# Seven-product FFN blocks from the second f block on, with GpSimd making their sums

## The chip, the cores and the metric

The kernel runs on one NeuronCore of a Trainium2 chip. The metric is the device time of one execution in microseconds (us). The engines have their names from the profile: PE (TensorE matmul) and PEld (its weight loads), DVE (VectorE), ACT (ScalarE), POOL (GpSimd) and SP (SyncE, which here only issues DMAs). SBUF is the on-chip memory, PSUM the accumulator that matmuls write.

## The reference, cut to what matters

The reference is two layers of a hybrid decoder: 16 learned tokens and 512 real ones (528 in all), width 1024, with an attention group and a retention group of heads in each layer and then a feed-forward part. The change touches the feed-forward part alone:

```python
hn = rmsnorm(h, ffn_norm_g)
ff = silu(hn @ w_gate) * (hn @ w_up)       # 1024 -> 2816, twice
return h + ff @ w_down                     # 2816 -> 1024
```

Layer 0 computes it for all 528 tokens, layer 1 only for the 512 real ones. All is float32. The kernel gets float32 accuracy from fast matmuls by splitting each operand into a high part (a rounded cast) and a low part (the rest): a product is three matmuls, high x high, high x low and low x high.

## The kernel before, in words

**Layout.** The residual `h` lies in SBUF as eight tiles `h[0..7]` of 128 features x 528 tokens. The 2816 hidden features of the FFN are 22 blocks of 128, called f blocks. For each f block, a gate matrix and an up matrix of 1024 x 128 are needed, each loaded by SP as one tile of 128 x 8 x 128.

**Plain f blocks** (`f < PLAIN`, lines 1031 to 1034). `dense_steps` (line 197) makes eight steps for the gate and eight for the up, one for each 128 input features: in layer 0 a step is six matmuls of 264 columns (three products, two halves of the tokens), in layer 1 three of 512. A block is 96 or 48 matmuls. The weights are cast by ACT (`whi`, line 191), and the low parts are made by DVE or, with `pool=True`, by POOL in eight pieces of 128 columns (line 194). Weights of the next matrix are made ahead at steps 1 and 4 of the current one. The high and low weight tiles are rings of two buffers.

**Seven-product f blocks** (class `Unit`, line 887). Gate and up are taken together as a 2 x 2 product of blocks: the 1024 inputs in two halves (rows), the tokens in two halves (columns). A Winograd form does it with seven half-size products in place of eight: 84 matmuls of 264 columns (256 in layer 1) for gate and up together. It needs sums of inputs and sums of weights:

- The token sums: `x_forms(k)` (line 834) for k = 0 to 3 makes, from `h[k]` and `h[k+4]`, four sums and differences in a tile `S`, and splits them into `th` (ACT) and `tl` (DVE). These serve all units of the layer. `S` is a ring of two buffers, so the third form can be started only when the first is split.
- The weight sums: `make1` to `make4` (lines 907 to 928). `make2` adds the two halves of up into `S[HB:NK]`, subtracts the gate's half, and splits the result (`splits`, lines 867 to 869); its tile comes from the same ring `S`. `make3` overwrites half of up in place.

A unit runs its `head` (24 matmuls on the ordinary inputs, no sums), its `middle` (36 matmuls on the token sums and on the tiles of `make2` and `make3`) and its `tail` (24). `need(j)` (line 862) makes a job's weights and those of up to two jobs after it when the first matmul of a product is reached. Round 0 holds f blocks 0 to 2; before the change all three are plain (`PLAIN = 3`), the units begin at f = 3, and from there on pieces of the down projection of the round before are put between the units.

**What sets the order.** PE runs in the order in which the Python steps are called. The other engines' orders are laid out by a planner at build time, by program order as priority, its own costs and the time at which tiles come free; after that each engine runs its queue strictly in order. The FFN's tiles lie in the memory that the attention tiles of the layer held.

**The start of the FFN.** `start_ffn` makes the scaled high and low inputs `xh`, `xl` (lines 311 to 324) from `h`. `ffn` then returns its list of steps, into which the last lines (1216 to 1220) insert other work by position: the squares for the norm before step 4; the norm (`rstd`, four or two matmuls), the held gate of block 0 and form 0 before step 12; forms 1, 2 and 3 before steps 20, 28 and 36. So the forms are spread over the three plain blocks.

Of the kernel before, what the change touches and what calls it, by code (L numbers as in the profile page):

```python
# [16 lines left out]
NK = D // 128  # L17
# [7 lines left out]
DFF = 2816  # L25
NF = DFF // 128
ROUNDS = ((0, 3), (3, 7), (7, 11), (11, 15), (15, 19), (19, 22))
PLAIN = 3
HB = NK // 2
EPS = 1e-6  # L30
NBLK = SEQ // 128
# [8 lines left out]
def hybrid_kernel(ctx, tc, x_t, w_in, w_fl, w_out, w_gate, w_up, w_down, vecs, b_fg, rope, decay, mask, ident, out_t):  # L40
# [232 lines left out]
    def fft(tag, dt=F32R, shape=(128, T), bufs=None):  # L273
        return phase["ffn"].tile(list(shape), dt, name=tag, tag=tag, bufs=bufs)
# [518 lines left out]
    def ffn(l, st, real, last):  # L793
# [14 lines left out]
        def g_done(f):  # L808
            def go(ps):
                sg = tt("sg")  # L810
                if isinstance(ps, list):
                    for v, (c0, c1) in zip(ps, QC):
                        nc.vector.scalar_tensor_tensor(sg[:, c0:c1], v[:, 0:c1 - c0], RSC, st["R"][:, c0:c1],
                                                       ALU.mult, ALU.mult)
                else:
                    nc.vector.scalar_tensor_tensor(sv(sg, real), pv(ps, real), RSC, sv(st["R"], real), ALU.mult, ALU.mult)
                silu(sv(sg, real))
                sgs[f] = sg
            return go

        def u_done(f):
            def go(ps):
                u = tt("tq")
                nc.vector.scalar_tensor_tensor(sv(u, real), pv(ps, real), RSC, sv(st["R"], real), ALU.mult, ALU.mult)
                nc.vector.tensor_mul(sv(u, real), sv(u, real), sv(sgs[f], real))
                fh, fl = act_tile(f)
                split(sv(fh, real), sv(fl, real), sv(u, real))
                acts[f] = (fh, fl)
            return go
# [4 lines left out]
        def x_forms(k):  # L834
            def go():
                if k == 0:
                    st["t"] = [[fft(f"t{p}{i}", shape=(128, 2, 4, w)) for p in "hl"] for i in range(2)]
                s = fft("S", F32, (128, 6, w), 2)
                a, b = ((h[k][:, c0:c1], h[HB + k][:, c0:c1]) for c0, c1 in HC)
                g0, g1 = vcol(V_FFN + l * NK + k), vcol(V_FFN + l * NK + HB + k)  # L840
                nc.scalar.activation(s[:, 0:2], two(h[k]), AF.Copy, scale=g0)
                nc.vector.tensor_sub(s[:, 2], s[:, 1], s[:, 0])
                for i in range(2):
                    nc.vector.scalar_tensor_tensor(s[:, 3 + i], b[1], g1, s[:, 1 + i], ALU.mult, ALU.subtract)
                nc.vector.scalar_tensor_tensor(s[:, 5], a[1], g1, s[:, 4], ALU.mult, ALU.subtract)
                th, tl = (t[:, k % 2] for t in st["t"][k // 2])
                split(th, tl, s[:, 2:6])
            return go
# [38 lines left out]
        class Unit:  # L887
# [23 lines left out]
            def make2(self, hi, lo):  # L911
                a, b = self.t["a"], self.t["b"]
                s = self.t["s"] = fft("S", F32, (128, NK, 128), 2)
                nc.vector.tensor_add(s[:, HB:NK], b[:, 0:HB], b[:, HB:NK])
                nc.vector.tensor_sub(s[:, 0:HB], s[:, HB:NK], a[:, 0:HB])
                splits(hi, lo, s)

# [111 lines left out]
        for r, (f0, f1) in enumerate(ROUNDS):  # L1029
            for f in range(f0, f1):  # L1030
                if f < PLAIN:
                    steps += dense_steps(w_gate[l, f], [(0, xs, NK, QC, g_done(f) if f else held.append)], banks=f == 1)
                    steps += dense_steps(w_up[l, f], [(0, xs, NK, QC, u_done(f))])
                    continue
                u = Unit(f)
                steps += u.head()
                for v in tails:
                    v.last()
                    steps += v.tail()
                tails = []  # L1040
                u.rest()
                steps += u.middle()
                if fills:
                    p, g0, g1 = fills.pop(0)
                    j = down_job(p, g0, g1)
                    steps += down(j, 0, 2 * p, g0, g1, not real)
                    u.last()
                    steps += u.tail()
                    steps += down(j, 1, 2 * p + 1, g0, g1, False)
                else:  # L1050
                    tails = [u]
            for p, g0, g1 in fills:
                j = down_job(p, g0, g1)
                for s in range(2):
                    steps += down(j, s, 2 * p + s, g0, g1, False)
            fills = [(p, f0, f1) for p in range(NK // 2)]
# [6 lines left out]
        else:  # L1063
# [149 lines left out]
            places = [(end, after_a)] + [(end + n * (i + 1), f) for i, f in enumerate(  # L1213
                (after_0, after_1, after_2, after_3, after_4, after_5, after_6, after_7))]
            steps += merge(rnd, places)
        for i in range(HB):
            steps.insert(NK + 4 + 9 * i, x_forms(i))
        steps.insert(NK + 4, lambda: g_done(0)(held[0]))
        steps.insert(NK + 4, lambda: rstd(st, QC))
        steps.insert(4, lambda: squares(st, QC, False, False))  # L1220
        return steps

    gf = const.tile([128, NK], F32, name="gf")
    nc.vector.tensor_scalar_mul(gf, vec[:, V_FIN:V_FIN + NK], RSC)
# [180 lines left out]
```

## Time and profile before

| | |
|---|---|
| median of 3 runs | 1274.08 us (1273.74 to 1275.27) |
| the profiled execution | 1278.19 us; its span 1276.3 us; mean granted PE clock 0.995 |
| first gate matmul of the FFN, layer 0 / layer 1 | 290.0 us / 918.0 us |
| three plain f blocks, layer 0 | from 290.0 to 325.6 us |
| POOL's additions of line 194 | 504 instructions, 259.9 us |
| POOL's busy time from 345 to 620 us (units of layer 0) | 0.38 us |
| DVE's busy time from 345 to 620 us | 220.33 us of 275 |
| DVE's busy time from 284 to 326 us | 41.93 us of 42 |

The profile is one execution. Its chain of work follows the wait that ended last at each point back from the end; the groups sum equal instructions with the mean time of one; the timeline and the windows show a stretch in order of time, in us from the span's start. In a timeline row the first number is the start, the second the time that it took; DVE instructions of 128 x 528 are listed with 0.70 us but start 0.62 us apart, since the next one starts before the last is written out. The ends of matmuls are modelled, so their starts are what to count by.

### The profile page before, as it was taken

What the parts mean: (1) busy time and instruction counts of PE and PEld (TensorE: products, weight loads), DVE (VectorE), ACT (ScalarE), POOL (GpSimd) and SP (SyncE); (2) the same over time, 40 slices, a digit from 0 to 9 for tenths busy, and PEclk for the clock granted to TensorE, in tenths of its full rate; (3) what the DMA queues carried; (4) which work ended last, traced back from release to release, by engine and by line L of the source; (5) the groups of instructions that cost most, each with busy time, mean ns of one, the idle gap of its engine ahead of it and who ended that gap; (6) DMA issues with size and microseconds to landing.
All of it is one profiled execution on the core that took longest, in us unless ns stands there. A gap on an engine that the chain in (4) does not pass through costs nothing.

```text
span 1276.3 us, 23615 instructions
## 1 busy us (share of the span) xinstructions
PE 1258.8 (99%) x9271; PEld 1199.9 (94%) x9271; DVE 996.6 (78%) x1843; ACT 688.2 (54%) x1246; POOL 265.2 (21%) x522
## 2 busy tenths in 40 slices
PE   9999999999999999999999999999999999999997
PEld 8899999999999999999998989999789999999996
DVE  7777856779988887887785777567899888888866
ACT  6666545676444444444464665456764444444444
POOL 3355546420000000000025545554100000000000
PEclk9999999999999999999999999999999999999998
DMA  6322232223333333332323232232224333333321
GB/s 216 93 68 84 79 94 72 74 67 112 108 96 100 100 100 100 100 100 83 102 74 100 76 100 84 75 92 67 99 86 129 100 100 100 100 99 101 106 76 67
DMA packets 45680, 120.57 MB, mean 94 GB/s; under 512 B 5360, under 2 KB 12272, under 8 KB 45568
## 3 DMA queue, kind: packets, MB, share of 16 engines
q1 hardware_dynamic: 45136, 118.77, 29.8%
q8 instruction: 73, 1.20, 0.4%
q14 instruction: 39, 0.32, 0.1%
q10 hardware_dynamic: 432, 0.29, 0.1%
HBM read 116.91 MB, written 2.13 MB: 93 GB/s over the span
## 4 chain that ended last, share of the span: by engine, by line
PE 94%; DVE 2%; ACT 1%; DMA 1%; issue 0%; DVEq 0%; ACTq 0%; SPq 0%
PE psd L217 30%; PE psa L880 18%; PE psd L1015 14%; PE psd L880 13%; PE psa L217 5%; PE psa L1015 4%; PE psa L418 2%; PE psa L572 2%; PE psa L507 2%; PE psa L729 1%; PE psa L699 1%; DMA bc<-cdr 1%; PE psa L379 1%; PE psa L290 0%; DMA cdr<-z 0%
## 5 line engine op out<-in xcount | busy, mean ns | idle before, releaser
L194 POOL TENSOR_TENSOR wlo<-raw,whi 128x128 fp32r<-128x128 f32 x504 | 259.9, 551 | 293.5 <-ACT whi L191 293.5
L217 PE MATMUL psd<-xh,whi 128*128 128x264 f32 (+1 forms) x792 | 197.1, 316 | 0.6 <-ACT whi L191 0.6
L217 PE MATMUL psd<-xh,wlo 128*128 128x264 f32 (+1 forms) x792 | 187.7, 305 | 0.0
L217 PE MATMUL psd<-xl,whi 128*128 128x264 f32 (+1 forms) x792 | 187.3, 304 | 0.4 <-DVE xl L320 0.4
L217 PEld LDWEIGHTS psd<-xh,whi 128*128 128x128 f32 x792 | 129.4, 191 | 5.7 <-ACT whi L191 1.3
L217 PEld LDWEIGHTS psd<-xh,wlo 128*128 128x128 f32 x792 | 128.0, 190 | 6.4 <-DVE wlo L194 0.4
L217 PEld LDWEIGHTS psd<-xl,whi 128*128 128x128 f32 x792 | 128.6, 190 | 4.8 <-DVE xl L320 0.8
L191 ACT CAST whi<-raw 128x512 fp32r<-128x512 f32 (+1 forms) x168 | 98.5, 614 | 51.6 <-PE psd L217 38.2
L868 ACT CAST whi<-raw 128x1024 fp32r<-128x1024 f32 (+2 forms) x62 | 54.9, 886 | 51.0 <-PE psd L880 39.5
L868 ACT CAST fwhi<-raw 128x1024 fp32r<-128x1024 f32 (+2 forms) x62 | 55.7, 898 | 46.6 <-PE psd L880 39.2
L1115 POOL TENSOR_TENSOR th<-th,e 128x544 f32<-128x544 f32 x1 | 1.4, 1370 | 359.1 <-DVE e L1135 359.1
L85 POOL MEMSET kl<- 64x528 f32 x2 | 1.1, 534 | 345.4 <-PE psa L880 345.4
L869 DVE TENSOR_TENSOR wlo<-raw,whi 128x1024 fp32r<-128x1024 f32 (+2 forms) x62 | 62.9, 1015 | 12.1 <-ACT whi L868 12.0
L869 DVE TENSOR_TENSOR fwlo<-raw,fwhi 128x1024 fp32r<-128x1024 f32 (+2 forms) x62 | 64.0, 1032 | 9.6 <-ACT fwhi L868 9.5
L880 PE MATMUL psa<-th,whi 128*128 128x264 f32 (+1 forms) x232 | 65.4, 282 | 0.0
L880 PE MATMUL psa<-th,wlo 128*128 128x264 f32 (+1 forms) x232 | 65.4, 282 | 0.0
L880 PE MATMUL psa<-tl,whi 128*128 128x264 f32 (+1 forms) x232 | 65.3, 282 | 0.0
L880 PE MATMUL psa<-th,fwhi 128*128 128x264 f32 (+1 forms) x224 | 63.4, 283 | 0.0
L880 PE MATMUL psa<-tl,fwhi 128*128 128x264 f32 (+1 forms) x224 | 63.3, 283 | 0.0
L880 PE MATMUL psa<-th,fwlo 128*128 128x264 f32 (+1 forms) x224 | 63.2, 282 | 0.0
L527 ACT ACTIVATE probs<-probs,nmax 128x144 f32<-128x144 f32 (+1 forms) x64 | 36.9, 577 | 47.3 <-DVE nmax L514 34.5
L868 ACT CAST fwhi<-S 128x1024 fp32r<-128x1024 f32 x20 | 21.0, 1050 | 69.1 <-PE psa L880 67.1
(340 smaller groups left out, 4053.7 us busy)
## 6 DMA issues: line engine op xcount, KB each, us to landing
raw<-w_in SPq DMA_DIRECT2D x54, 512.0 KB, 3.5
raw<-w_gate SPq DMA_DIRECT2D x44, 512.0 KB, 3.8
fraw<-w_up SPq DMA_DIRECT2D x38, 512.0 KB, 3.5
raw<-w_down SPq DMA_DIRECT2D x64, 256.0 KB, 2.8
raw<-w_out SPq DMA_DIRECT2D x16, 512.0 KB, 3.4
raw<-w_down SPq DMA_DIRECT2D x32, 192.0 KB, 2.5
bc<-cdr SPq DMA_DIRECT2D x16, 264.0 KB, 3.4
raw<-w_up SPq DMA_DIRECT2D x6, 512.0 KB, 3.6
```

The lines of the kernel that those rows point to most:

```text
L191: pin(nc.scalar.copy(hi, job["raw"][:, c0:c1]), pinned)
L194: pin(sub(lo[:, i:i + step], job["raw"][:, c0 + i:c0 + i + step], hi[:, i:i + step].bitcast(F32)), pinned)
L217: nc.tensor.matmul(ps[1][b][:, 0:c1 - c0], w[:, wk, :], x[:, c0:c1], start=(k == 0 and i == 0), stop=(k == n - 1 and i == 2))
L379: nc.tensor.matmul(ps[:, 0:c1 - c0], wf[:, k, :], st["x"][k][part][:, c0:c1], start=(i == 0), stop=(i == 2 * NK - 1))
L418: nc.tensor.transpose(ps[:, 128 * j:128 * j + 128], src[:, o:o + 128], idt)
L507: nc.tensor.matmul(sc[0:nq, 0:c1 - c0], st["q"][s][:, q0:q0 + nq], kk[:, c0:c1], start=(i == 0), stop=(i == 1))
L527: nc.scalar.activation(pr, pr, AF.Exp, bias=nmax[0:nq], scale=-1.0, accum_out=rsum)
L572: nc.tensor.matmul(po[:, c0:SEQ], v[:, j, :], pp[:, j, META + c0:T], start=(j == 0 and i == 0), stop=(j == 4 and i == 1))
L868: nc.scalar.copy(hi, src)
L869: nc.vector.tensor_sub(lo, src, hi.bitcast(F32))
L880: nc.tensor.matmul(bank()[:, 0:b.shape[-1]], a[:, o + k, :], b, start=(fresh and k == 0 and i == 0), stop=(k == n - 1 and i == 2), skip_gr ...
L1015: nc.tensor.matmul(v[:, 0:c1 - c0], a[:, s * n + k, :], b[:, c0:c1], start=(k == 0 and i == 0), stop=(k == n - 1 and i == 2))
```

## The change

`PLAIN` goes from 3 to 1: f blocks 1 and 2 of each layer become units, so four blocks in all. The four forms are now placed before steps 5, 7, 9 and 11 of the one plain block (16 steps), and the norm before step 11. In a form, ACT scales both `h[k]` and `h[k+4]` into `S` (which has eight parts now), and the four sums are subtractions of 264 or 256 columns on POOL; before, they were one subtraction and three fused operations on DVE. The plain block's up has its low parts made by POOL, eight pieces of 128 columns. In `make2` of every unit (42 now, 38 before) the sum of the up halves is four POOL additions of 128 columns in place of one DVE addition of 512. Transfers and their sizes stay as they were.

```diff
-PLAIN = 3
+PLAIN = 1
...
-                s = fft("S", F32, (128, 6, w), 2)
-                a, b = ((h[k][:, c0:c1], h[HB + k][:, c0:c1]) for c0, c1 in HC)
+                s = fft("S", F32, (128, 8, w), 2)
                 g0, g1 = vcol(V_FFN + l * NK + k), vcol(V_FFN + l * NK + HB + k)
                 nc.scalar.activation(s[:, 0:2], two(h[k]), AF.Copy, scale=g0)
-                nc.vector.tensor_sub(s[:, 2], s[:, 1], s[:, 0])
+                nc.scalar.activation(s[:, 6:8], two(h[HB + k]), AF.Copy, scale=g1)
+                nc.gpsimd.tensor_sub(s[:, 2], s[:, 1], s[:, 0])
                 for i in range(2):
-                    nc.vector.scalar_tensor_tensor(s[:, 3 + i], b[1], g1, s[:, 1 + i], ALU.mult, ALU.subtract)
-                nc.vector.scalar_tensor_tensor(s[:, 5], a[1], g1, s[:, 4], ALU.mult, ALU.subtract)
+                    nc.gpsimd.tensor_sub(s[:, 3 + i], s[:, 7], s[:, 1 + i])
+                nc.gpsimd.tensor_sub(s[:, 5], s[:, 6], s[:, 4])
                 th, tl = (t[:, k % 2] for t in st["t"][k // 2])
                 split(th, tl, s[:, 2:6])
...
                 s = self.t["s"] = fft("S", F32, (128, NK, 128), 2)
-                nc.vector.tensor_add(s[:, HB:NK], b[:, 0:HB], b[:, HB:NK])
+                for i in range(HB):
+                    nc.gpsimd.tensor_add(s[:, HB + i], b[:, i], b[:, HB + i])
                 nc.vector.tensor_sub(s[:, 0:HB], s[:, HB:NK], a[:, 0:HB])
                 splits(hi, lo, s)
...
                 if f < PLAIN:
-                    steps += dense_steps(w_gate[l, f], [(0, xs, NK, QC, g_done(f) if f else held.append)], banks=f == 1)
-                    steps += dense_steps(w_up[l, f], [(0, xs, NK, QC, u_done(f))])
+                    steps += dense_steps(w_gate[l, f], [(0, xs, NK, QC, g_done(f) if f else held.append)], f > 0, f == 1)
+                    steps += dense_steps(w_up[l, f], [(0, xs, NK, QC, u_done(f))], True)
...
-        for i in range(HB):
-            steps.insert(NK + 4 + 9 * i, x_forms(i))
-        steps.insert(NK + 4, lambda: g_done(0)(held[0]))
-        steps.insert(NK + 4, lambda: rstd(st, QC))
-        steps.insert(4, lambda: squares(st, QC, False, False))
-        return steps
+        forms = (5, 7, 9, 11)
+        return merge(steps, [(4, lambda: squares(st, QC, False, False)), (NK + 3, lambda: rstd(st, QC)),
+                             (NK + 3, lambda: g_done(0)(held[0]))], [(p, x_forms(i)) for i, p in enumerate(forms)])
```

## The prediction

> **What bounds the kernel now.** I read the page first: the busy shares, the slices, the chain that ended last.
>
> ```profile
> PE 1258.8 (99%) x9271; PEld 1199.9 (94%) x9271; DVE 996.6 (78%) x1843; ACT 688.2 (54%) x1246; POOL 265.2 (21%) x522
> ...
> DVE  7777856779988887887785777567899888888866
> ...
> POOL 3355546420000000000025545554100000000000
> ...
> PE 94%; DVE 2%; ACT 1%; DMA 1%; issue 0%; DVEq 0%; ACTq 0%; SPq 0%
> ```
>
> PE is the bound: 94% of the chain is its own work. So fewer matmuls gain what they take, and work shifted between DVE and POOL gains nothing unless PE waited for it; it can cost. DVE is fullest (9 tenths) where each FFN starts; POOL does nothing in the FFNs. Next I read the chain of waits in time over the start of the FFN, layer 0 and then layer 1 (start, length, what).
>
> ```profile
> 302.58 5.79 PE psa L217 x48
> 308.37 17.36 PE psd L217 x144
> 325.73 1.45 PE psa L880 x12
> ...
> 918.05 1.14 ACT whi L191 x2
> 919.19 1.24 ACT S L841 x2
> 920.43 0.61 ACT xh L319
> ...
> 930.66 5.52 PE psa L217 x24
> 936.19 16.59 PE psd L217 x72
> 952.77 1.43 PE psa L880 x12
> ```
>
> L217 is a plain block, L880 a unit. In layer 0 PE runs three plain blocks without a wait of note; in layer 1 ACT's scaled copies for two forms stood ahead of `xh` and reached the chain.
>
> **The gain in matmuls.** Layer 0: 144 plain matmuls take 17.36 us, 0.1206 each; a block of 96 takes 11.57. Twelve unit matmuls take 1.45; the 84 take 10.15. Gain 1.42 a block, 2.8 for two. Layer 1: 72 in 16.59 is 0.2304, a block of 48 takes 11.06; 7 x 1.43 = 10.01; gain 1.05 a block, 2.1 for two. Together 4.9 us, 0.4% of the kernel, if PE never waits.
>
> **When PE wants the first weight sums.** Before, unit 3 came behind three plain blocks; now unit 1 comes behind one. Its head (24 matmuls, 2.9 us) needs no sums; its middle needs all four token sums and the tile of `make2`. In layer 0 block 1 began at 302.58, so the middle is wanted at 305.5; in layer 1 block 1 began at 930.66, plus 2.85: 933.5.
>
> **When POOL can have them.** POOL gets 8 low parts of the plain up, 16 subtractions, and 4 additions of `make2`, in program order. The source view and the groups of instructions give POOL's prices:
>
> ```profile
> L194 POOL TENSOR_TENSOR wlo<-raw,whi x504: 447/463/2071, 21.9 to 902.8; 128x128 fp32r<-128x128 f32 x168
> L1115 POOL TENSOR_TENSOR th<-th,e 128x544 f32<-128x544 f32 x1 | 1.4, 1370 | 359.1 <-DVE e L1135 359.1
> ```
>
> The timelines of ACT and DVE give the earliest start and the other links:
>
> ```profile
> 289.98 1.15 ACT L191 CAST whi<-raw 128x512 fp32r<-128x512 f32 x2 [0.63 <-PE psd L217]
> 291.03 0.74 ACT L841 ACTIVATE S<-h,vec 128x528 f32<-128x528 f32 x1
> 300.31 1.07 ACT L142 CAST th<-S 128x1056 fp32r<-128x1056 f32 x1
> 322.83 1.06 ACT L868 CAST fwhi<-S 128x1024 fp32r<-128x1024 f32 x1 [1.03 <-DVE S L915]
> 301.42 1.26 DVE L143 TENSOR_TENSOR tl<-S,th 128x1056 fp32r<-128x1056 f32 x1
> 322.11 0.69 DVE L915 TENSOR_TENSOR S<-S,raw 128x512 f32<-128x512 f32 x1
> 323.92 1.23 DVE L869 TENSOR_TENSOR fwlo<-S,fwhi 128x1024 fp32r<-128x1024 f32 x1
> ```
>
> One piece of 128 columns is 0.45 to 0.46 us undisturbed (447 least, 463 median). 264 columns on POOL are not in the trace. Between 463 ns at 128 and 1370 at 544 a column costs 2.18 ns, so 264 cost an estimated 0.76 and 256 0.74. Bounds: 0.46, the same price as 128, and 1.37, the row of 544; I take the value between, which the two rows fix.
>
> [...]
>
> The up's cast could begin at 289.98 because PE had then let go of the weight ring; ACT copied the first form's `S` only behind it, at 291.03, with gaps in its queue before. So I read the FFN's `S` memory as coming free with the last out projection. Walk in layer 0, POOL never disturbed:
> - 8 low parts from 290.6, when half of the cast is done: 8 x 0.45, to 294.2.
> - Forms 0 and 1: 4 x 0.76 = 3.04 each, to 297.2 and 300.2.
> - Form 2 needs form 0's buffer: `th` 1.07 and `tl` 1.26 after 297.2, then its copy 0.74: 300.3. It runs to 303.3, form 3 to 306.3.
> - `make2` of unit 1 needs a buffer of `S` too, the one of form 2 (305.7), and stands behind form 3: 4 x 0.45 to 308.1; DVE's subtraction 0.69, ACT's cast 1.06: high part at 309.9; low part 1.23 later, 311.1.
>
> PE issues two matmuls with the high part (0.24 us) and stops for the low: wanted at 305.7, there at 311.1. Loss 5.4. In layer 1 the same walk, from 918.6 (the cast began at 918.05) with 0.74 a sum, ends at 938.9 against 933.7: 5.2. So undisturbed POOL alone loses 10.6 us, more than twice the gain.
>
> **POOL disturbed.** DVE is full there (window over the plain block of layer 0: span, then PE, PEld, DVE, ACT, POOL busy), and POOL and DVE are seen to hold each other up (their timelines in the attention, the group of all POOL pieces, DVE's timeline ahead of the gate):
>
> ```profile
> 290.02:302.20 12.18, 12.18 (x101) 12.03 (x100) 12.14 (x22) 7.94 (x14) 0.00 (x0) 1.00 0.63 212
> 85.09 4.42 POOL L194 TENSOR_TENSOR wlo<-raw,whi 128x128 fp32r<-128x128 f32 x6 [4.62 <-ACT whi L191]
> 86.57 0.85 DVE L758 TENSOR_TENSOR d<-d,sg 128x528 f32<-128x528 f32 x1
> 87.34 0.96 DVE L452 TENSOR_TENSOR kl<-tq,kh 64x528 fp32r<-64x528 f32 x1
> 88.23 0.96 DVE L297 TENSOR_TENSOR nwt<-r 128x528 f32<-128x528 f32 x1
> L194 POOL TENSOR_TENSOR wlo<-raw,whi 128x128 fp32r<-128x128 f32 x504 | 259.9, 551 | 293.5 <-ACT whi L191 293.5
> 291.09 2.12 DVE L320 SCALAR_TENSOR_TENSOR xl<-h,vec,xh 128x528 fp32r<-128x528 f32 x3
> 293.75 1.44 DVE L320 SCALAR_TENSOR_TENSOR xl<-h,vec,xh 128x528 fp32r<-128x528 f32 x2
> ```
>
> Six POOL pieces that should take 2.7 us take 4.42, and DVE's neighbours, all with two SBUF inputs, follow each other 0.77 to 0.89 us apart. Over the kernel a POOL piece takes 551 ns on average, 0.09 over the median: 28 instructions pay 2.5 us. The other end is that each meets a DVE instruction and waits some 0.3 to 0.4 more: 28 x 0.35 is 9.8. DVE has less to do than before (the twelve fused operations are gone), but what remains, `xl`, `tl` and weight lows, has two SBUF inputs. I take 3 us a layer, near the mean row. The other way DVE pays: the last two `xl` (1.44 us from 293.75) were just in time for PE, and the POOL pieces now beside them may delay gate steps by about 1 us; that stays in the range, as do 0 to 1.3 us for two more `S` copies ahead of `xh` in ACT's queue.
>
> [...]
>
> **PE's clock.** A PE that stands still runs slower afterwards:
>
> ```profile
> 680.00:686.00 6.00, 3.61 (x16) 2.78 (x15) 3.99 (x15) 2.96 (x11) 1.70 (x4) 0.79 0.34 117
> ```
>
> With PE idle for 2.4 of 6 us the granted clock averaged 0.79, a loss of about 0.21 x 6 = 1.3 us of matmul time. For a stop of 8 us I add 1.5 in each layer; from 0 (it falls while PE stands anyway) to 3.
>
> **What costs nothing.** The later units hide their POOL additions (a steady unit of layer 0: DVE's, ACT's and PE's rows):
>
> ```profile
> 501.98 0.69 DVE L914 TENSOR_TENSOR S<-fraw 128x512 f32<-128x512 f32 x1 [0.72 <-DMA fraw<-w_up]
> 508.24 1.05 ACT L868 CAST fwhi<-S 128x1024 fp32r<-128x1024 f32 x1 [4.20 <-PE psa L880]
> 512.39 1.46 PE psa L880 x12
> ```
>
> The addition starts when its load lands, 6.3 us before ACT may cast (it waits for a weight buffer from PE), and PE needs it after the head (2.9 us from 512.39), 13 us on. Four additions of 0.45, or 3.2 if each is disturbed as above, and the 0.69 of the subtraction fit. Queued behind that subtraction on DVE are `make3` in place (it must also let the additions read first) and evictions; were the cover gone, each of 38 units would pay up to 3 us. DVE's relief (an addition of some 0.69 a unit, the form work) frees no PE wait. The weight loads are the same bytes; those of units 1 and 2 replace the plain blocks' in the same places.
>
> **The sum.** Gain 4.9; walk 10.6; disturbance 2 x 3 = 6.0; clock 2 x 1.5 = 3.0: 10.6 + 6.0 + 3.0 - 4.9 = 14.7 us slower. On the profiled execution's 1278.19 that is 1292.9; that execution lies 4.1 above the median of 1274.08, so the median comes to 1288.8.
>
> **The rivals.**
> - *Faster: the sums are there in time.* If the `S` memory is free before 290, ACT copies forms 0 to 2 as their `h` arrive and POOL, idle at that point, does 9 us of subtractions ahead of the gate. It decides at POOL's first subtraction: from some 5.4 us before the walk's 294.2, so at about 289, the wait is gone. For it: the out projection completes most tiles of `h` before the gate begins. Against it: in both layers ACT copied `S` only behind the up's casts. Time: 1274.1 - 4.9 = 1269.2. Chance 0.15.
> - *No change.* The sums come 2.5 us late in each layer (a cheaper POOL column: the lower bound of 0.46 takes 16 x 0.30 = 4.8 off a layer's walk, and disturbance gives about half of it back): 1274. Chance 0.06.
> - *Units bound by their sums.* The POOL additions, each held up by DVE's long low-part instructions, push `make2` past ACT's slot in every unit: some 0.4 us in each of 42 on top of the forecast, 17 us: 1306. For it: DVE at 8 tenths there. Against it: the 4.2 us that ACT waits. Chance 0.05.
> - That the change does not do what it says can be left out: the count of matmuls follows from the steps.
>
> **How the numbers follow.** Forecast 0.74: slower by 6 (no disturbance, no clock: 10.6 - 4.9) to 28 us (9.8 a layer, 3 a layer of clock), so 1280 to 1302. The range goes down to 1272, taking in no change, and leaves out most of the faster case and of the last. Differences below 0.2% (2.5 us) are about what a measurement of this kernel cannot tell from none. Faster 0.15, same 0.06, slower 0.79.
>
> **What would show it.** In the profile after: PE idle ahead of the first L880 on `th` with the weights of `S`, some 5 to 11 us in each layer, its releaser ACT's cast or DVE's low part of `S`; POOL busy without a gap from about 291 to 310 with pieces well over 0.46; POOL subtractions of 264 near 0.76; a drop of the granted clock behind the wait; units from f = 3 on without PE waits. I am wrong if POOL's subtractions begin before 289, or if PE has no wait there.

## The result, and the profile after

The changed kernel takes 1315.88 us (median of 4 runs, 1314.7 to 1317.35) against 1274.67 for the kernel before on the same chip: a ratio of 1.0323, 95% interval 1.0305 to 1.0341. It is 41 us slower. The prediction was 14.7 slower, with a range that ended at 1302. The direction was right and the size was not.

The profiled execution took 1317.35 us, with a span of 1315.6. Below are the page's busy line, two of the slice lines and the engines' shares of the chain, as they were shown of the kernel before.

```profile
PE 1265.8 (96%) x9319; PEld 1206.9 (92%) x9319; DVE 989.1 (75%) x1792; ACT 701.8 (53%) x1266; POOL 428.0 (33%) x738
...
POOL 3445645436222111110034545454442111211100
PEclk9999999997999999999999999999978999999999
...
PE 83%; DVE 7%; POOL 3%; ACT 3%; issue 1%; DMA 1%; DVEq 0%; ACTq 0%; SPq 0%; POOLq 0%
```

PE's own work went from 94% to 83% of the chain; DVE, POOL and ACT stand on it now. The clock has a dip at the start of each layer's FFN. PE's matmuls date the loss. From the first gate matmul to the first down product (the first matmul of the down projection), a stretch with the same three f blocks and the head and middle of unit 3, the profiled executions took:

| us | layer 0 | layer 1 |
|---|---|---|
| before | 42.79 | 41.64 |
| after | 59.29 | 59.37 |
| from the first down product to the FFN's end, before | 314.87 | 304.47 |
| the same, after | 316.51 | 310.44 |

That is 16.5 + 17.7 in the first stretch and 1.6 + 6.0 behind it, 41.8 of a difference of 39.2 between the two profiled executions; the other stretches are 2.6 shorter. So the loss is where the prediction looked, but more than twice as large in each layer (7.1 was predicted for layer 0: 5.4 + 3 + 1.5 - 2.8).

The windows view over that stretch (us, then busy us and instructions of PE, PEld, DVE, ACT and POOL, then the granted clock, DMA share and GB/s), layer 0, before and after:

```profile
290.02:332.81 42.79, 42.79 (x355) 42.64 (x354) 42.38 (x70) 26.48 (x39) 0.00 (x0) 1.00 0.38 120
```

```profile
288.68:347.97 59.29, 44.51 (x330) 43.20 (x329) 45.45 (x57) 33.48 (x48) 33.48 (x40) 0.86 0.27 85
```

Read the first row twice: PE was busy for all of 42.79 us, and DVE for 42.38 of them. Two engines were full, and the swap of the blocks takes work from one of them only. Afterwards neither is full; everything waits on something. PE's rows that have a wait ahead of them from unit 1 on, from the timeline of layer 0 after:

```profile
303.24 0.39 PE L880 MATMUL psa<-xh,wlo 128*128 128x264 f32 x1 [0.90 <-DVE wlo L869]
...
314.36 0.56 PE L880 MATMUL psd<-xh,whi 128*128 128x264 f32 x1 [9.63 <-DVE sg L816]
...
319.70 0.59 PE L880 MATMUL psa<-th,fwhi 128*128 128x264 f32 x1 [2.36 <-ACT fwhi L868]
...
321.76 0.59 PE L880 MATMUL psa<-th,fwlo 128*128 128x264 f32 x1 [1.25 <-DVE fwlo L869]
```

The long stop is one that the prediction did not have: unit 1's head wants a PSUM bank for its `z` tile, and the bank is still held by block 0's gate, which waits for the norm `R`. The wait for the weight sums that the prediction described comes behind it, 2.4 + 1.3 us. In layer 1 PE stops 10.63 us for the same bank and then finds the sums just made. The chain that ended last shows why both are late (start, length, what):

```profile
289.39 6.73 POOL wlo L194 x8
296.12 0.71 POOL S L842
296.83 1.44 POOL S L844 x2
...
300.10 0.74 ACT S L841
...
300.91 2.90 POOL S L844 x2
...
304.66 1.07 ACT th L142
305.73 0.75 ACT R L295 x2
306.49 0.63 ACT S L841
...
307.19 1.92 POOL S L844 x2
...
309.94 1.08 ACT th L142
...
311.05 1.26 DVE tl L143
312.31 1.17 DVE R L300
...
313.50 0.71 DVE sg L816
```

The chain runs through POOL's forms into ACT's `th` and DVE's `tl`, and from `tl` straight into `R` at 312.31: the norm does not need the forms, but it stands behind them in ACT's and DVE's queues. ACT's second copy of a form, `S` of line 841, stands behind `th` in the same way, and POOL waits for it.

### The profile page after: what moved, and what is told of

Same layout as the page of the kernel before. It is cut to its first block, busy times and chain, and to the rows that moved or that the text cites. A ratio compares the mean times of both kernels' runs of the same rounds, so it can differ in the third digit from the quotient of the medians.

```text
span 1315.6 us, 23991 instructions
## 1 busy us (share of the span) xinstructions
PE 1265.8 (96%) x9319; PEld 1206.9 (92%) x9319; DVE 989.1 (75%) x1792; ACT 701.8 (53%) x1266; POOL 428.0 (33%) x738
## 4 chain that ended last, share of the span: by engine, by line
PE 83%; DVE 7%; POOL 3%; ACT 3%; issue 1%; DMA 1%; DVEq 0%; ACTq 0%; SPq 0%; POOLq 0%
PE psd L217 23%; PE psa L880 19%; PE psd L880 13%; PE psd L1016 13%; PE psa L1016 4%; PE psa L217 4%; PE psa L418 2%; PE psa L572 2%; PE psa L507 1%; PE psa L729 1%; PE psa L699 1%; POOL S L844 1%; POOL wlo L194 1%; POOL S L915 1%; PE psa L379 1%
## 5 line engine op out<-in xcount | busy, mean ns | idle before, releaser
L194 POOL TENSOR_TENSOR wlo<-raw,whi 128x128 fp32r<-128x128 f32 x520 | 272.5, 558 | 323.9 <-ACT whi L191 323.8
L915 POOL TENSOR_TENSOR S<-fraw 128x128 f32<-128x128 f32 x168 | 121.3, 753 | 447.9 <-DMA fraw<-w_up 424.4
L217 PE MATMUL psd<-xh,whi 128*128 128x264 f32 (+1 forms) x720 | 177.8, 316 | 0.5 <-ACT whi L191 0.5
L217 PE MATMUL psd<-xl,whi 128*128 128x264 f32 (+1 forms) x720 | 168.7, 303 | 1.4 <-DVE xl L320 1.4
L217 PE MATMUL psd<-xh,wlo 128*128 128x264 f32 (+1 forms) x720 | 168.1, 302 | 0.0
L217 PEld LDWEIGHTS psd<-xl,whi 128*128 128x128 f32 x720 | 116.4, 190 | 6.1 <-DVE xl L320 3.2
L217 PEld LDWEIGHTS psd<-xh,whi 128*128 128x128 f32 x720 | 117.1, 191 | 4.7 <-ACT whi L191 1.2
L217 PEld LDWEIGHTS psd<-xh,wlo 128*128 128x128 f32 x720 | 115.8, 189 | 4.8
L880 PE MATMUL psa<-th,wlo 128*128 128x264 f32 (+1 forms) x264 | 75.1, 284 | 0.3 <-DVE wlo L869 0.3
L880 PE MATMUL psd<-xh,whi 128*128 128x264 f32 (+1 forms) x176 | 51.6, 293 | 20.3 <-DVE sg L816 20.3
L947 ACT COPY e<-psa 128x264 f32<-128x264 f32 (+1 forms) x126 | 47.3, 375 | 33.6 <-PE psa L880 27.7
```

The lines of the kernel that those rows point to most:

```text
L194: pin(sub(lo[:, i:i + step], job["raw"][:, c0 + i:c0 + i + step], hi[:, i:i + step].bitcast(F32)), pinned)
L217: nc.tensor.matmul(ps[1][b][:, 0:c1 - c0], w[:, wk, :], x[:, c0:c1], start=(k == 0 and i == 0), stop=(k == n - 1 and i == 2))
L880: nc.tensor.matmul(bank()[:, 0:b.shape[-1]], a[:, o + k, :], b, start=(fresh and k == 0 and i == 0), stop=(k == n - 1 and i == 2), skip_gr ...
L915: nc.gpsimd.tensor_add(s[:, HB + i], b[:, i], b[:, HB + i])
L947: nc.scalar.copy(self.t["e"][:, i], self.t["x"][:, 0:w])
```

## The experiments

Four causes were weighed. P, the prediction's own: POOL's sums are late and its instructions and DVE's hold each other up. D: DVE was already full, and a unit gives it more work than a plain block. G, the hand-over: the last unit of round 0 ends its activations too late for the first down product, because its tail is put off into the next unit. C, the queues: work that needs no sums waits in order behind `th` and `tl`, which wait for POOL. Each ratio is to the kernel before on the same chip in the same session, and a difference of two runs in us is that of their ratios, or of their times where they were taken together.

### Is it POOL at all?

plain1_dve keeps one plain block and the new positions, and does everything on DVE as before.

```diff
-PLAIN = 3
+PLAIN = 1
...
+        forms = (5, 7, 9, 11)
```

> One plain block per layer and the forms at steps 5 to 11 as in the change, but every sum and low part on DVE as before; POOL does nothing in the FFN. Theory A (POOL's chain, stretched by DVE, makes the sums late): DVE alone needs from 295.7 us about 1.2 (lows) + 6.2 (forms) + 4.7 (tl) + 3.7 (norm, held gate) + 1.1 + 2.3 (weights of unit 1) = 19 us, so the first weight sums come some 9 us late instead of the change's 16 to 18: about 1288, some 25 us under the change. Theory B (PE stops for the PSUM bank of the held gate, wherever the sums are made): the norm still queues behind four forms, so nearly the same stop: 1308 to 1316.

Measured: 1308.61 us, ratio 1.0260 (1.0243 to 1.0277). The same swap loses 33 us with no work on POOL. The time is one that theory B named, but not by its mechanism: PE's wait for the held gate's bank is down to 3.40 us in layer 0, and 6.08 + 0.45 us are waits for the weight sums. The window of layer 0's stretch, and DVE's rows around the first weight sum:

```profile
288.90:342.76 53.86, 43.93 (x330) 42.99 (x329) 49.87 (x78) 30.47 (x44) 0.00 (x0) 0.90 0.29 94
```

```profile
309.26 2.42 DVE L143 TENSOR_TENSOR tl<-S,th 128x1056 fp32r<-128x1056 f32 x2
311.60 0.70 DVE L143 TENSOR_TENSOR al<-tq,ah 128x528 fp32r<-128x528 f32 x1
312.22 1.28 DVE L914 TENSOR_TENSOR S<-fraw 128x512 f32<-128x512 f32 x2
313.42 0.68 DVE L915 TENSOR_TENSOR S<-S,raw 128x512 f32<-128x512 f32 x1
```

DVE has 49.87 us to do where it had 42.38, and it runs without a gap of note until 321.7; unit 1's sum waits its turn there and is done at 314, where PE wanted it at about 309. forms_dve takes the changed kernel and puts only the forms back on DVE; the up's low parts and the additions stay on POOL.

```diff
-                nc.gpsimd.tensor_sub(s[:, 2], s[:, 1], s[:, 0])
+                nc.vector.tensor_sub(s[:, 2], s[:, 1], s[:, 0])
...
```

> The change with the four forms back on DVE (the six-part S); the up's low parts and the weight sums stay on POOL. Theory A: POOL's chain shrinks from 28 us to 8 lows (6.7) and 4 additions (2.8), DVE takes 6.2 us of forms: first sums some 9 to 10 us late, about 1288 to 1292. Theory B: as the change, 1308 to 1316.

Measured: 1309.74, ratio 1.0272 (1.0254 to 1.0289). With the low parts and additions on POOL the time is 1 us longer than plain1_dve's, which the intervals cannot tell from none, and with the forms there too 6 us more. The 33 us of plain1_dve are not a part of the changed kernel's 41, though: in the one DVE makes the forms, in the other DVE is rid of them and waits for POOL (4.43 us ahead of the first `tl`). Each kernel has its own chain, and both are late.

### What the swap runs into

plain2_dve swaps one block only, all sums on DVE.

```diff
-PLAIN = 3
+PLAIN = 2
...
+        forms = (12, 16, 20, 24)
```

> Two plain blocks per layer, everything on DVE as before, the forms at steps 12, 16, 20 and 24. Theory D (DVE is full from the first gate to the first down product, and a plain block turned into a unit adds some 3.7 us of DVE work to it while PE's work shrinks by 1.2): a loss of 3.4 us a layer plus some clock, 1280 to 1288. Theory E (the chain of the first weight sums alone decides: with 11.6 us more cover they are there in time): 1272 to 1275.

Measured: 1291.81, ratio 1.0132 (1.0117 to 1.0147): half of plain1_dve's loss for half of the swap, and somewhat more than either theory had. Layer 0 shows G in PE's and DVE's timelines:

```profile
340.28 0.63 PE L1015 MATMUL psa<-ah,fwhi 128*128 128x264 f32 x2 [2.31 <-ACT ah L142]
341.56 0.81 PE L1015 MATMUL psa<-al,fwhi 128*128 128x264 f32 x2 [0.65 <-DVE al L143]
```

```profile
337.24 0.42 DVE L949 TENSOR_TENSOR e<-psd,e 128x264 f32<-128x264 f32 x1
...
339.14 0.42 DVE L964 TENSOR_TENSOR tq<-e,tq 128x264 f32<-128x264 f32 x1
...
340.81 0.70 DVE L143 TENSOR_TENSOR al<-tq,ah 128x528 fp32r<-128x528 f32 x1
```

The down product gets through two f blocks and stops at the third, whose activations are just being made. Before, block 2 was plain and done well ahead of unit 3. plain2_tail moves the tail:

```diff
+                elif f == f1 - 1:
+                    u.last()
+                    steps += u.tail()
                 else:
                     tails = [u]
```

> Two plain blocks, all sums on DVE, as in plain2_dve (1291.81), but the last unit of round 0 runs its tail behind its own middle and not inside the next unit, so that its activations are started some 36 matmuls earlier against the first down product. Theory G (the hand-over: PE stops at the first down product for activations that are late because the tail was put off): 4 to 8 us less a kernel, 1283 to 1288. Rival D alone (DVE's queue is full, so what is saved at this wait comes back as another one): 1290 to 1294.

Measured: 1286.96, ratio 1.0086 (1.0071 to 1.0102), 0.46% less than plain2_dve: G holds. The same edit in the changed kernel:

> The changed kernel with the tail of round 0's last unit behind its own middle, nothing else. If the hand-over (G) is a loss of its own there, 1308 to 1312. If the late sums and the late norm hide it, as the short waits at the first down product suggest (0.9 us in layer 0, 2.8 in layer 1), 1313 to 1317.

Measured: 1312.09, ratio 1.0282 (1.0267 to 1.0298), 0.41% or 5 us less than after. The short waits had suggested otherwise; the gain is in the stretch behind the first down product, which falls from 310.44 to 304.75 us in layer 1.

plain1_nosums takes DVE's form work out of plain1_dve; ACT fills `S` alone, and the token sums are left out.

```diff
-                nc.scalar.activation(s[:, 0:2], two(h[k]), AF.Copy, scale=g0)
-                nc.vector.tensor_sub(s[:, 2], s[:, 1], s[:, 0])
-                for i in range(2):
-                    nc.vector.scalar_tensor_tensor(s[:, 3 + i], b[1], g1, s[:, 1 + i], ALU.mult, ALU.subtract)
-                nc.vector.scalar_tensor_tensor(s[:, 5], a[1], g1, s[:, 4], ALU.mult, ALU.subtract)
+                nc.scalar.activation(s[:, 2:4], two(h[k]), AF.Copy, scale=g0)
+                nc.scalar.activation(s[:, 4:6], two(h[HB + k]), AF.Copy, scale=g1)
```

> plain1_dve without the forms' subtractions: ACT fills S with scaled copies and nothing is subtracted, so the token sums are left out; splits and everything behind stay. It takes 6.2 us a layer off DVE. Theory D (DVE's work in the first stage is the bound): 12 us or more under plain1_dve's 1308.6, so 1288 to 1297. If not DVE's work but the order of waits in the chain holds PE up: within 4 us of 1308.6.

Measured: 1286.01, ratio 1.0087 (1.0072 to 1.0102), 22 us below plain1_dve. D holds for the kernel with its sums on DVE. The subtractions are listed with 7.2 us of DVE a layer (before: 3.6 + 1.9 + 1.7 in their groups) and fill 6.2 by their starts, and the first stretch is 9.1 and 8.2 us shorter than plain1_dve's; the rest of the 22 lies behind the first down product. The gain is more than the 12.4 us of work that the edit removes from both layers. `th` no longer waits for DVE either, and what that alone is worth was not parted from the work. nosums_tail adds the early tail:

> One plain block, the forms' subtractions left out (ACT alone fills S, the token sums are not computed), as in plain1_nosums (1286.01), with the tail of round 0's last unit behind its own middle. If DVE's added work (D) and the hand-over to the down projection (G) are together the whole loss of plain1_dve (1308.61), this kernel comes to 1272 to 1280, since the two extra units also save PE some 5 us. If a third cause is left, 1283 to 1287.

Measured: 1282.49, ratio 1.0050 (1.0035 to 1.0065), so a third cause was left. nosums_tail_tl was to take 4 x 1.26 us more from DVE by filling `tl` on ACT:

> nosums_tail (1282.49, 1.0050 of before; one plain block, token sums left out, tail early) with the low parts of the forms filled by ACT as well, so that DVE loses four more instructions of 1.26 us in each layer. DVE is busy there for 44.77 of the 47.09 us between the first gate matmul and the first down product of layer 0. If DVE's queue is what is left of the loss (D), this saves 4 to 8 us of the kernel: 1274 to 1279. If another cause is left (the units' order of casts and PSUM turns on PE and ACT), 1281 to 1284.

Measured: 1288.88, ratio 1.0089 (1.0072 to 1.0106). Neither time came, and D was not tested: ACT then ran without a gap from 288.9 to 312.9, and the first cast of weight sums stood in that queue until 309.5. nosums_no_tl leaves `tl` out without loading another engine:

```diff
-            return lambda k: [t[:, k % 2, i] for t in st["t"][k // 2]]
+            return lambda k: [st["t"][k // 2][0][:, k % 2, i]] * 2
```

> nosums_tail (1282.49, 1.0050 of before: one plain block, token sums left out, tail early) without the low parts of the token sums at all: tl is neither made nor stored, and the products read th in its place, so PE's and ACT's instructions stay as they were and DVE loses four of 1.26 us in each layer. nosums_tail_tl (1288.88) had given that work to ACT, which then ran without a gap until the first weight sums' cast, so it told nothing of DVE. If DVE's queue is what is left of the loss (D): 4 to 8 us less, 1274 to 1279. If it is the chain of each unit's weight sums from ring to ring (U: cast, low part, matmuls and the next cast, with nothing between units 1, 2 and 3 to cover it): 1280 to 1284.

Measured: 1280.97, ratio 1.0042 (1.0027 to 1.0056), hardly less. The profile says why: PE's waits for weight sums are gone, and one wait has grown from 1.6 us (nosums_tail) to:

```profile
304.87 0.36 PE L876 MATMUL psd<-xh,whi 128*128 128x264 f32 x1 [3.05 <-DVE sg L816]
```

This is the held gate's bank. On the changed kernel, the held gate in single banks, so that unit 1 need not wait for it:

```diff
-    steps += dense_steps(w_gate[l, f], [...], f > 0, f == 1)
+    steps += dense_steps(w_gate[l, f], [...], f > 0, f <= 1)
```

> The change with the held gate of block 0 in psa banks, so that unit 1's z tile needs no bank of the held gate; in layer 1 the bank wait is then gone (in layer 0 the x bank waits instead, since four psa banks are full). Theory A: the stop in layer 1 moves to the first matmul on the weight sums and keeps its end; the time stays at 1313 to 1319. Theory B: layer 1 gains its 10.6 us: 1305 to 1308.

Measured: 1315.49, ratio 1.0316 (1.0297 to 1.0334): nothing, since the sums and the norm were late as well, and the stop moved to them (7.0 us for the norm's bank and 5.7 for `fwhi` in layer 0). Now that they are not, the same edit on nosums_no_tl:

> nosums_no_tl (1280.97, 1.0042 of before: one plain block, no token sums, no tl, tail early) with the held gate of block 0 in single banks, so that unit 1's z tile needn't wait for it. In nosums_no_tl PE's waits for the sums are gone and one is left: 3.1 and 2.5 us for the held gate's bank, with half the clock for 3.4 us behind it. If that is the rest of the loss (H: with one plain block the norm, and so the held gate, ends behind the point where unit 1 wants its bank), 5 to 8 us less: 1272 to 1276, below before for the first time. If the stop moves to another tile, as it did in gate_banks, 1279 to 1282.

Measured: 1274.57, ratio 0.9992 (0.9983 to 1.0002); 0.5% or 6.4 us less than nosums_no_tl. One short wait is left ahead of unit 1:

```profile
288.03:330.17 42.14, 40.61 (x331) 40.04 (x329) 38.72 (x59) 32.45 (x48) 0.00 (x0) 1.00 0.34 112
```

```profile
301.63 0.36 PE L876 MATMUL psa<-xh,whi 128*128 128x264 f32 x1 [1.07 <-DVE nwt L299]
```

So plain1_dve's loss is three limits, one behind the other: DVE's queue, the hand-over, and the held gate's bank. With all DVE work on the token sums left out the swap only breaks even: layer 0's stretch is 42.14 us where 2.8 us less PE work should make it 40.0. Waits of 1.07 and 0.47 us are seen in it; the other half microsecond was not followed.

### What POOL costs where there is time

pool_covered leaves three plain blocks and the old positions, and gives POOL the forms, block 0's up low parts and the units' additions.

```diff
-PLAIN = 1
+PLAIN = 3
...
-        forms = (5, 7, 9, 11)
+        forms = (12, 20, 28, 36)
```

> Three plain blocks again with the forms spread at their old places, but POOL does what the change gives it: the forms' subtractions, the low parts of block 0's up, the additions in every unit. Theory A: 23 us more cover hide a POOL chain of 28 us; what is left is the slip of the gate by xl (1 to 2 us a layer): 1275 to 1279. If the additions in the steady units cost PE time (rival), 38 units would show it: 1285 or more.

Measured: 1295.35, ratio 1.0157 (1.0138 to 1.0176). Theory A fell: with all the cover of before, POOL's work costs 20 us. The time fits the rival, POOL's additions in the 38 units, but they are not it: behind the first down product the FFNs take 315.29 and 304.49 us, as before the change (314.87 and 304.47), and the loss lies in the first stretches, 53.55 and 51.52 us for 42.79 and 41.64. PE waited there for the held gate, 6.66 us in layer 0, and ACT's timeline shows what held it:

```profile
298.51 1.08 ACT L142 CAST th<-S 128x1056 fp32r<-128x1056 f32 x1 [5.31 <-POOL S L845]
...
303.85 1.07 ACT L142 CAST th<-S 128x1056 fp32r<-128x1056 f32 x1 [2.60 <-POOL S L845]
...
306.10 0.83 ACT L295 ACTIVATE R<-psa,epsc 128x264 f32<-128x264 f32 x2
```

ACT stands idle at `th`, and `R` comes behind. pool_pinned kept `th` and `tl` behind the work traced before them:

```diff
-                split(th, tl, s[:, 2:6])
+                split(th, tl, s[:, 2:6], True)
```

> pool_covered with one thing changed: on ACT and DVE the forms' splits stand behind the norm and the held gate in the queues, where pool_covered has two of them ahead. Theory C (in-order queues: the norm waits behind splits that wait for POOL, the held gate keeps its PSUM bank and PE stops): the waits for the held gate (9.9 us) and the half clock behind them go, 1276 to 1281. Theory A' (POOL and DVE delay each other whatever the order): no change from 1295, or 1290 and more.

Measured: 1296.78, ratio 1.0168 (1.0152 to 1.0184). It decided nothing: the pin holds only behind the previous ACT instruction, which was the form's own copy, so `th` stood ahead of `R` as before. pool_after_norm pins the first copy behind the held gate:

```diff
-                nc.scalar.activation(s[:, 0:2], two(h[k]), AF.Copy, scale=g0)
+                pin(nc.scalar.activation(s[:, 0:2], two(h[k]), AF.Copy, scale=g0), k == 0)
```

> Three plain blocks, GpSimd doing the forms, block 0's up low parts and the units' additions, as in pool_covered (1295.35), but ACT's first copy of the forms now stands behind the held gate's silu in ACT's queue, so no link of the forms can stand ahead of the norm on ACT or DVE. Theory C (the loss with cover is the norm and the held gate queued behind th and tl that wait for POOL): the held gate's bank comes free as before the change, PE's wait for it (9.9 us in layer 0) goes, 1276 to 1283. Rival A' (POOL's work itself, and the DVE instructions that it holds up, set the loss wherever they stand): 1288 or more, with DVE's low parts and POOL's pieces still near 0.9 us.

Measured: 1296.97, ratio 1.0166 (1.0148 to 1.0184). By its time this is A', the rival in which POOL and DVE delay each other whatever the order. But the profile shows C with another victim. `R` is on time, at 298.11, and the wait for the held gate is gone; now the plain weights' casts stand behind `th`:

```profile
312.10 1.07 ACT L142 CAST th<-S 128x1056 fp32r<-128x1056 f32 x1 [2.07 <-POOL S L845]
...
313.63 0.60 ACT L191 CAST whi<-raw 128x512 fp32r<-128x512 f32 x1
```

pool_split_late parts the two. `th` and `tl` become steps of their own, 9 to 14 steps behind their form's copies and subtractions, and are pinned there; forms 1 to 3 also start 6 to 8 steps earlier than in pool_covered:

```diff
+                st["s", k] = s
+            return go
+
+        def x_split(k):
+            def go():
...
-                split(th, tl, s[:, 2:6])
+                split(th, tl, st["s", k][:, 2:6], True)
...
-        forms = (12, 20, 28, 36)
+        forms = (12, 13, 22, 28)
+        splits_at = (21, 27, 34, 39)
...
```

> Three plain blocks and GpSimd's work as in pool_covered (1295.35), but each form is cut in two: its copies and POOL's subtractions stand 6 to 12 steps ahead of its th and tl, which are pinned behind the work traced before them. So ACT and DVE should reach th and tl only when POOL has finished. Theory C' (the loss with cover is what is queued in order behind th and tl while these wait for POOL: the norm in pool_covered, the plain weights' casts in pool_after_norm): the waits of th for POOL, some 8 to 10 us of ACT's time in layer 0, go to under 3, and the time comes to 1276 to 1283. Rival A' (POOL's pieces and the DVE instructions that meet them set the loss wherever th stands): 1288 or more.

Measured: 1281.85, ratio 1.0039 (1.0024 to 1.0054). ACT's waits of `th` for POOL between 287 and 326 us (us in all, times, the longest), from the views of waits of pool_after_norm and of pool_split_late; pool_covered has 12.1:

```profile
ACT th L142 <- POOL S L845: 10.0, 4, 3.1
```

```profile
ACT th L142 <- POOL S L845: 1.3, 1, 1.3
```

About 15 of pool_covered's 20 us go when the forms start earlier and `th` and `tl` stand later, so that nothing waits behind them for POOL. The 5 that stay hold the disturbance between POOL and DVE and what the new positions cost; these two were not parted. The same edit in the changed kernel, with its one plain block, was not run.

### Whether the clock cost anything

keep_warm adds 104 unused matmuls to unit 1 of the changed kernel, 80 ahead of the long stop and 24 ahead of the sums.

```diff
+                    for _ in range(n):
+                        nc.tensor.matmul(ps[:, 0:w], ones, st["x"][0][0][:, t0:t0 + w], start=True, stop=True)
```

> The change with 80 idle matmuls in the middle of unit 1's head and 24 ahead of its middle in each layer (results unused), in the time in which PE stands: about 9.7 and 2.9 us of PE work in waits of 9.9 to 10.6 and 2.8 us. Theory F (the half clock behind the waits costs time): the granted clock stays at 1 there, 4 to 10 us under the change: 1306 to 1312. If the clock costs nothing because other engines are late anyway: 1314 to 1318.

Measured: 1318.03, ratio 1.0348 (1.0326 to 1.0370), no gain. The same window of layer 0, after and keep_warm:

```profile
308.00:325.10 17.10, 7.13 (x29) 6.55 (x30) 13.73 (x16) 9.20 (x12) 11.34 (x14) 0.50 0.04 6
```

```profile
308.00:325.10 17.10, 14.82 (x105) 14.19 (x103) 13.71 (x16) 9.49 (x13) 10.33 (x13) 0.90 0.09 29
```

The clock went from 0.50 to 0.90 and nothing came of it: PE was not what the others waited for. The added matmuls did not hold PE up in layer 0, where it still waited 0.58 and 1.55 us for the weight sums behind them; for layer 1 this was not shown.

## Why the prediction was right in direction and wrong in size

- **Right: one plain block is too little cover, and POOL's order.** The prices held: an undisturbed subtraction of 264 columns took 0.75 us (estimate 0.76), and POOL began at 289.39, with no gap until form 1. POOL made low parts, forms and additions in the order walked. The direction is in part luck: plain1_dve, with no walk on POOL at all, loses 33 us.
- **Right: later units hide their additions.** From 361.5 to 636.5 us POOL was busy for 45.65 us, and PE for all 275.00:

```profile
361.50:636.50 275.00, 275.00 (x2262) 275.00 (x2261) 210.40 (x309) 122.19 (x173) 45.65 (x64) 1.00 0.32 97
```

- **Wrong, the step that failed: the walk to the first weight sums, with 3 us a layer on top for the disturbance.** It took every link at its price and let ACT and DVE take up each one at once. Layer 0, us from the first gate matmul:

| | walked | measured |
|---|---|---|
| POOL begins | 0.6 | 0.7 |
| form 3 ends on POOL | 16.3 | 26.2 |
| the low part of `make2`'s tile is there | 21.1 | 33.0 |
| PE could want it | 15.7 | |
| late by | 5.4, and 3.0 for the disturbance | 17.4 |

  In layer 1 it was 17.5 for 5.2 and 3.0. Together that is 34.9 us late where the sum had 16.6. Less the 4.9 us of matmuls this leaves 30.0 of the 39.2 us between the profiled executions; the other 9.2 are net of all the rest, with 7.6 behind the first down products. gate_banks bears it out: with the norm's bank out of the way the stop moved to these sums and the time stayed. No run took the lateness itself away from the changed kernel; that account is read from its trace.
- **The parts of the 17.4 us.** The groups of POOL from 285 to 348 us, beside the estimates of 0.45 and 0.76:

```profile
L844 POOL TENSOR_TENSOR S<-S 128x264 f32<-128x264 f32 x8 | 8.6, 1094 | 4.1 <-ACT S L841 4.1
L194 POOL TENSOR_TENSOR wlo<-raw,whi 128x128 fp32r<-128x128 f32 x8 | 6.7, 874 | 16.5 <-ACT whi L191 16.5
L845 POOL TENSOR_TENSOR S<-S 128x264 f32<-128x264 f32 x4 | 3.0, 748 | 0.3
L842 POOL TENSOR_TENSOR S<-S 128x264 f32<-128x264 f32 x4 | 3.0, 746 | 0.0
```

  Against 0.45 and 0.75 apiece, the low parts and `L844` lost 3.1 and 2.6 us. Another 4.1 are POOL's gaps, waiting for ACT's second copy `S`, which stood behind `th`: a link that the walk had not. That is what form 3 was late. Behind it, `make2`'s additions took 2.76 us for 1.8, and DVE's two rows lost some 0.5 and began 0.6 late behind other work. So the disturbance was about 7 us for 3, and the order of ACT's and DVE's queues about 5 us for nothing.
- **Wrong by omission: what else is queued behind `th` and `tl`.** The walk followed who feeds the sums, and not who stands behind them on ACT and DVE. The norm stood there, and so the first and longest stop was for a PSUM bank, before the sums were even asked for. It cost nothing by itself (gate_banks), because the sums were as late. The forms on POOL are 6 us of the loss against the forms on DVE; with three plain blocks POOL's work costs 20.
- **Wrong by omission: DVE's balance.** "DVE's relief ... frees no PE wait" looks at what leaves DVE, and "DVE has less to do than before" leaves out what the units bring. The prediction showed DVE busy for 12.14 of 12.18 us in the plain block and used that only for the disturbance. A plain block gives DVE four low parts and four steps on gate and up, 0.61 us each by their starts, 4.9 in all; a unit's rows come to nearly twice that. By the windows of layer 0 plain1_dve's DVE has 49.87 - 42.38 = 7.5 us more for two units. So a swap takes 1.05 to 1.42 us from PE and puts 3.7 on an engine that had 0.41 us to spare in the stretch: some 7 us lost in each layer if DVE keeps the sums. In the changed kernel they have left DVE, which is busy for 45.45 of 59.29 us there, so its sum is not the bound. The offload traded a full DVE for a late POOL: 33 us lost the one way, 41 the other.
- **Wrong by omission: the hand-over.** That the last unit of a round ends inside the next one is in the kernel's code (`tails = [u]`, line 1051), but the walk stopped at the sums of unit 1. It costs 5 us (after_tail).
- **Wrong: the clock.** 3 us were charged for it. Half the clock lasted 17.07 us in layer 0, much longer than assumed, and cost nothing there (keep_warm). The size was wrong in one direction, the price in the other.
- **The range.** Its upper end was given as 28 us slower, from 9.8 us of disturbance and 3 of clock a layer. The 9.8 was an estimate, 0.35 us more for each of 28 POOL instructions; in layer 0 they lost about 6.7 us (3.1 + 2.6 + 1.0, from the parts above). With the walk and the gain these add up to 10.6 + 19.6 + 6.0 - 4.9 = 31.3, so 1305; the measured time lies above that too.
- **The rivals.** The faster one's point of decision was POOL's first subtraction before 289; it came at 296.08. No change asked for sums 2.5 us late; they were 17.4. Units bound by their sums did not occur.

No version here beats the kernel before. The nearest, no_tl_banks, leaves work out and only equals it.

## What to carry to other kernels

Before swapping a block for one with less matmul work, set up the sum for each engine over that stage: where a second engine is as full as PE, the swap is bought at that engine's price. A walk along a chain needs, at each link, what stands ahead of it in that engine's queue. When work goes to a slower engine (a subtraction of 264 columns took 0.75 us on POOL and 0.42 on DVE), ask who stands in order behind the instructions that take its results, and part the producer from its consumer by other work (pool_split_late) before judging the engine. And when an edit that removes one wait gives nothing, look whether the stop has moved: single banks for the held gate gave nothing in gate_banks and 6.4 us in no_tl_banks.

## What the runs showed of the hardware

**POOL and DVE held each other up, both ways.** In layer 0 after, DVE beside POOL's eight low parts:

```profile
289.74 2.53 DVE L320 SCALAR_TENSOR_TENSOR xl<-h,vec,xh 128x528 fp32r<-128x528 f32 x3
292.20 0.96 DVE L340 TENSOR_TENSOR ss<-ss,sq 128x528 f32<-128x528 f32 x1
293.08 1.84 DVE L320 SCALAR_TENSOR_TENSOR xl<-h,vec,xh 128x528 fp32r<-128x528 f32 x2
```

The same rows before the change were 2.12 for the three `xl` and 1.44 for the two; `ss` was 0.70. POOL's pieces took 874 ns where 447 is the least. They did not simply take turns: alone, the eight pieces (8 x 0.447 us) and these six DVE instructions (2.12 + 0.70 + 1.44) take 7.8 us, and all were done within POOL's 6.73. From the end of the low parts, while DVE stood idle for 4.43 us, POOL's subtractions took 0.75 each. What DVE paid differed from one instruction to the next. Beside POOL's subtractions until 314.06, `R`, with both inputs in SBUF, took 1.25 us where it had 0.70, and `sg<-psd,R`, which follows it and has one input in PSUM, 0.71 where it had 0.70. `tl` at 316.03, with both inputs in SBUF, took the 1.26 us that it took at 305.77 with POOL idle; the POOL piece beside it took 1.51 where the three ahead of it took 0.46 each.

**Half the clock came in steps of 3.41 us, and a little over half a step of idle PE was enough.** In the traces of before and after, between 60 and 1262 us, the stretches at 0.50 were 3.41, 6.83, 13.65 and 17.07 us long. In after the stretches at full clock between two of them were 375.47, 242.35, 6.83 and 27.31 us, so all these changes of the clock lie on one grid of 3.41 us. PE's busy time in the steps of that grid, with the modelled ends of the matmuls: in the step ahead of each fall 1.02 us in before and 0.10, 1.62, 0.81, 0.56 and 1.64 in after, and in every other step at full clock 2.49 or more. A step at half the clock with 2.48 us busy or less was followed by another one, a step with 3.34 or more by the full clock. No step lay between these values. In nosums_tail's layer 0 no single wait of PE was longer than 1.7 us (1.6, 1.7, 0.8 and 0.5), and PE ran at half the clock while it was busy all the time:

```profile
310.40:313.80 3.40, 3.40 (x18) 3.40 (x17) 3.37 (x5) 1.06 (x3) 0.00 (x0) 0.50 0.39 142
```

plain1_nosums had waits of 1.5, 1.7, 0.8 and 0.9 us there, and its clock from 289 to 333.8 us was 1.00. What parts these two was not followed. In the traces of before and after it was PE's busy share of a step that went with the fall, 48% and less of the 3.41 us.
